# Last token block of a hybrid layer: mixer rows loaded early into a pool of their own, and the sums of its first weights made beside the early blocks

## The chip, the cores and the metric

The kernel runs on one core of a Trainium2 chip. The core has TensorE (PE, matrix multiply; PEld is its weight load), VectorE (DVE), ScalarE (ACT), GpSimd (POOL) and SyncE (SP), which here only issues DMAs. Each takes its instructions in order. Times are device microseconds of the whole kernel; lower is better.

## What is computed

One layer of a hybrid encoder on 17 tiles of up to 128 tokens (16 of the prompt, one of 64 sample tokens), model width 1024. Three mixers (Mamba-2, RWKV-7, HGRN2) scan the tokens in order; their joined output y goes through an output projection, then a SwiGLU feed-forward network (FFN):

```python
y = concatenate([y_ssd, y_rw, y_hg], axis=-1)
x = x + y @ w_out
h = rmsnorm(x, norm2_w)
x = x + (silu(h @ w_gate) * (h @ w_up)) @ w_down
out = rmsnorm(x, final_norm_w)
```

Every product is made of float32 values split into a high and a low part (hi, lo) of a reduced type, with three multiplies in place of one: hi·hi, lo·hi, hi·lo.

## The kernel before

**Blocks.** The projection and FFN run over blocks of tokens. Three early blocks of three tiles each (EARLY: 0-2, 3-5, 6-8; class Ffn) run out() (output projection, norm), ffn() (22 column groups f of gate, up and down) and rest() (the final norm of each tile). Beside them the mixers of later tiles are worked off as streams. The late block (LATE, eight tiles, halves h of four tiles j) comes after all mixers: it does its projections by one level of Strassen-Winograd, seven products (PRODS) of half-size sub-matrices in place of eight. Their right operands are quarters of the weights (b11 to b22) and sums of them (t1 to t4); their left ones are quarters of the rows (a11 to a22) and sums (s1 to s4).

**Order.** A scheduler in the build sets the order of instructions on each engine from the program and the dependencies of tiles. What can be placed early depends on the tiles' pools: a pool opened at the addresses of one that was closed waits for the last users of those addresses.

**Weights.** Weight units come through two small rings. "raw" has three tiles of 256 KB (128x512 float32), "w" five of 512 KB (hi and lo). The first early block splits the units and keeps them in DRAM; later blocks load them ready (w<-w, line 214). Sums of weights are made by t_sums (lines 1308 to 1327): four quarters are loaded into raw tiles on SP, summed, and the four results go to DRAM on POOL's queue. For the output projection ("wo", six groups) the program places them in the last early block (out_prep), for w_down ("wd", eleven) after each pair; both use POOL for the arithmetic. When needed, a sum is loaded again and split by parts().

**Late block, step by step.** After the last early block: the ya tiles (y of the three mixers, 24 loads, line 1427), the residual rows acc and the norm's row nw are loaded on SP. Op tiles (to_parts, lines 1405 and 1406: a copy on ACT and a subtraction on VectorE) feed the output projection, tokens_first("wo"). second_half works on the rows of the second half while the projection still runs, first_half(j) on those of the first: transposes (line 1464, d<-ident,w2k), sums and parts of them. Then come eleven pairs (gate and up columns): columns() yields after each of its seven products, x, y and z are PSUM banks, and c tiles hold copies and sums. Two pairs are stepped ahead by two products each. The results' seven combinations are stored (ms and ma, on POOL's queue). At the end m_group loads them into mraw for tokens_first("wd"), acc comes back from DRAM (xs), and final_norm writes the outputs.

final_norm (lines 1125 to 1136) squares a row on ACT into a w2k tile h, writes the normalised row over the same tile, and stores from there.

Of the kernel before, what the change touches and what calls it, by code (L numbers as in the profile page):

```python
# [19 lines left out]
P = 128  # L20
D = 1024
# [27 lines left out]
NH = 4  # L49
TAIL = 4  # L50
# [26 lines left out]
def body(tc, A, O, blocks=None, supers=None, dbg=None):  # L77
# [1047 lines left out]
    def final_norm(p, xt, t, n, fw, h):  # L1125

        s2 = mk(p, [P, 2], tag="s2", bufs=2)
        ss = mk(p, [P, 1], tag="ss", bufs=2)
        for hf in range(2):
            S.activation(h[hf][:n], xt[:, hf * 512:hf * 512 + 512], AF.Square, accum_out=s2[:n, hf:hf + 1])  # L1130
        V.tensor_tensor(ss[:n], s2[:n, 0:1], s2[:n, 1:2], ADD)
        rs = inv_rms(p, ss, n, 1, 1.0 / D, EPS)
        for hf in range(2):
            cs = slice(hf * 512, hf * 512 + 512)
            V.scalar_tensor_tensor(h[hf][:n], xt[:, cs], rs[:n], fw[:n, cs], MUL, MUL)
            G.dma_start(O["y_prompt"][(t - 1) * P:t * P, cs] if t else O["y_sample"][:, cs], h[hf][:n])

    class Ffn:
# [134 lines left out]
        def final(self, i, fw):  # L1273
            t, n = self.tiles[i], self.lens[i]
            final_norm(self.fp, self.acc[:n, i, :], t, n, fw, [self.w2k(), self.w2k()])

    if supers:
# [4 lines left out]
        def early():  # L1282
            drain(ALLY(EARLY[0]))
            fs[0].start()
            for i, f in enumerate(fs):
                drain(ALLY(EARLY[i]))
                yield from f.out()
                if i + 1 < len(fs):
# [3 lines left out]
                    yield from f.ffn(NFF - AHEAD, NFF)  # L1292
                else:
# [13 lines left out]
        def t_sums(key, q, p, tag, bufs, eng):  # L1307

            def ld(n):
                r = mk(p, [P, 512], tag=tag, bufs=bufs)  # L1310
# [8 lines left out]
            eng.tensor_tensor(a, a, b, SUB)  # L1319
            st("t3", a)  # L1320
            c_ = ld(0)
            eng.tensor_tensor(b, b, c_, SUB)
            st("t1", b)
            eng.tensor_tensor(c_, a, c_, ADD)
            st("t2", c_)
            d_ = ld(2)
            eng.tensor_tensor(d_, d_, c_, SUB)
            st("t4", d_)

        def quarters(key, kk):  # L1330
            if key == "wo":
# [9 lines left out]
        def parts(raw, eng):  # L1341
# [3 lines left out]
            eng.tensor_tensor(lo, raw, wt[:, 0], SUB)  # L1345
            return hi, lo

        def b_tm(key, kk, n):
# [5 lines left out]
            return parts(raw, V)  # L1354
# [5 lines left out]
        def tokens_first(key, order, per, group, acc, then, ahead, behind):  # L1360
# [3 lines left out]
            for a, b, x, fresh, (h, d) in PRODS:  # L1364
                if fresh:
                    banks[x] = [(xbank if x == 0 else ybank)() for _ in range(NH)]
                ps = banks[x]
                add = lambda j: V.tensor_tensor(acc[h][:, j, d * 512:d * 512 + 512], ps[j],
                                                acc[h][:, j, d * 512:d * 512 + 512], ADD)
# [12 lines left out]
                for g0 in range(0, len(order), per):  # L1382
                    kks = order[g0:g0 + per]
                    op = ops.get(g0) or group(a, kks)
                    for i, kk in enumerate(kks):
                        wu = b_tm(key, kk, b)
# [13 lines left out]
        def op_tile(tag="op"):  # L1400
            o = mk(lq, [P, 2, 4, 512], F32, tag=tag, bufs=4 if tag == "op" else 3)
# [5 lines left out]

        flow(early())
# [6 lines left out]
        lq = pool(st, "lq", side="right", reuse_waits="tile")  # L1415
        tile_of = lambda h, j: LATE[h][j]
        xs2 = [dram.tile([P, NH, D], F32, tag=f"xs{h}", name=f"xs{h}") for h in range(2)]

# [3 lines left out]
        ya = {}  # L1422
        for m in (2, 0, 1):
            ya[m] = mk(lq, [P, 2, 4, 512], F32, tag="ya", bufs=3)
            for h in range(2):
                for j in range(NH):
                    nc.sync.dma_start(ya[m][:, h, :, j * P:j * P + P], yscr[m][tile_of(h, j)])  # L1427
        acc = [mk(lo_, [P, NH, D], tag=f"acc{h}", bufs=1) for h in (1, 0)][::-1]
        for h in range(2):
# [26 lines left out]
        def scaled(h, j):  # L1456
            hs[h, j] = [mk(lo_, [P, 512], tag="w2k", bufs=4) for _ in range(2)]
            rms_scaled(lo_, acc[h][:, j, :], P, nw, hs[h, j])
            G.dma_start(xs2[h][:, j, :], acc[h][:, j, :])
# [55 lines left out]
        def columns(w, i):  # L1515

            raw = {}
            for n, f, k in (("22", 1, 1), ("12", 1, 0), ("11", 0, 0), ("21", 0, 1)):
                raw[n] = mk(lp, [P, 512], tag="lraw", bufs=16)
                nc.sync.dma_start(raw[n], w[2 * i + f][:, k * 512:k * 512 + 512])  # L1520
            V.tensor_tensor(raw["22"], raw["22"], raw["12"], SUB)
            V.tensor_tensor(raw["12"], raw["12"], raw["11"], SUB)
            V.tensor_tensor(raw["11"], raw["22"], raw["11"], ADD)
            V.tensor_tensor(raw["21"], raw["21"], raw["11"], SUB)
            raw = {"t3": raw["22"], "t1": raw["12"], "t2": raw["11"], "t4": raw["21"]}

            def prod(ps, a, b, first=True):
                if b in raw:
                    hi, lo = parts(raw[b], V)
                else:  # L1530
                    f, k = int(b[2]) - 1, int(b[1]) - 1
                    hi, lo = load_unit(w[2 * i + f][:, k * 512:k * 512 + 512])
# [7 lines left out]
            def copy(tag, ps):  # L1540
                r = mk(lp, [P, 512], tag=tag, bufs=4)
# [211 lines left out]
```

## Time and profile before

| | us |
|---|---|
| runs of the kernel, median of three | 3619.61 |
| lowest, highest | 3611.94, 3636.17 |
| profiled execution | 3608.43 |
| its span (mean clock 0.97) | 3606.7 |
| TensorE busy | 3373.3 |
| VectorE, ScalarE, GpSimd busy | 2199.1, 1238.1, 794.7 |

Times in a row of the profile are from the span's start. A row of the timeline has start, duration, engine, line, operation, output<-inputs, shapes, count, and in brackets the engine's idle time before it with what ended it. In rows of groups the part behind the bar is busy time and mean of one in ns. PEclk is the granted clock of TensorE as a share of full speed; DMA share is the load of the 16 DMA engines.

### The profile page before, as it was taken

What the parts mean: (1) busy time and instruction counts of PE and PEld (TensorE: products, weight loads), DVE (VectorE), ACT (ScalarE), POOL (GpSimd) and SP (SyncE); (2) the same over time, 40 slices, a digit from 0 to 9 for tenths busy, and PEclk for the clock granted to TensorE, in tenths of its full rate; (3) what the DMA queues carried; (4) which work ended last, traced back from release to release, by engine and by line L of the source; (5) the groups of instructions that cost most, each with busy time, mean ns of one, the idle gap of its engine ahead of it and who ended that gap; (6) DMA issues with size and microseconds to landing.
All of it is one profiled execution on the core that took longest, in us unless ns stands there. A gap on an engine that the chain in (4) does not pass through costs nothing.

```text
span 3606.7 us, 60714 instructions
## 1 busy us (share of the span) xinstructions
PE 3373.3 (94%) x22588; PEld 2951.2 (82%) x22588; DVE 2199.1 (61%) x4866; ACT 1238.1 (34%) x2618; POOL 794.7 (22%) x1048
## 2 busy tenths in 40 slices
PE   7999999999999998989888999999997969999798
PEld 7998689889799996778777889879996757888586
DVE  3358456558766677687776666766435775554353
ACT  4445333344433444434342222322102432333231
POOL 3325202102111123345444200111000343010001
PEclk9999999999999999899999999999999979999899
DMA  9776865555666668789888867777778678564756
GB/s 316 233 221 220 287 213 173 159 171 176 240 213 179 202 206 303 262 282 322 290 313 306 280 221 241 232 258 232 222 254 263 221 241 284 175 194 142 261 188 207
DMA packets 424256, 847.80 MB, mean 235 GB/s; under 512 B 111233, under 2 KB 211081, under 8 KB 419865
## 3 DMA queue, kind: packets, MB, share of 16 engines
q1 hardware_dynamic: 404024, 778.37, 65.8%
q0 software_dynamic: 19936, 65.55, 4.8%
q8 instruction: 178, 2.92, 0.3%
q14 instruction: 118, 0.96, 0.1%
HBM read 597.52 MB, written 246.25 MB: 234 GB/s over the span
## 4 chain that ended last, share of the span: by engine, by line
PE 43%; DMA 13%; issue 11%; DVE 8%; POOL 4%; SPq 2%; ACT 1%; POOLq 0%; DVEq 0%; ACTq 0%
PE g L109 32%; PE d L109 3%; PE c L109 3%; PE h L109 3%; DMA raw<-in_w_down 2%; DMA w<-w 2%; DMA raw<-in_w_gate 1%; POOL w L220 1%; DMA raw<-in_w_up 1%; DVE tp L638 1%; DVE Xp L639 1%; SPq L1427 1%; DMA raw<-in_w_out 1%; DMA b4k<-psc 1%; POOL ms L1599 1%
## 5 line engine op out<-in xcount | busy, mean ns | idle before, releaser
L109 PE MATMUL g<-hhi,w 128*128 128x384 f32 (+3 forms) x3312 | 833.6, 330 | 12.6 <-DMA w<-w 4.4
L109 PEld LDWEIGHTS g<-hhi,w 128*128 128x128 f32 (+1 forms) x3312 | 579.7, 188 | 28.5 <-DMA w<-w 4.1
L109 PE MATMUL g<-h2hi,w 128*128 128x384 f32 (+1 forms) x2112 | 544.0, 334 | 7.9 <-ACT w L218 3.3
L109 PE MATMUL g<-hlo,w 128*128 128x384 f32 (+3 forms) x1680 | 549.9, 328 | 0.0
L109 PEld LDWEIGHTS g<-h2hi,w 128*128 128x128 f32 x2112 | 374.6, 189 | 18.0 <-ACT w L218 4.8
L109 PE MATMUL g<-h2lo,w 128*128 128x384 f32 (+1 forms) x1056 | 349.1, 331 | 1.1 <-DVE h2lo L253 1.1
L220 POOL TENSOR_TENSOR w<-raw,w 128x512 fp32r<-128x512 f32 x180 | 247.9, 1380 | 343.4 <-ACT w L218 303.4
L109 PEld LDWEIGHTS g<-hlo,w 128*128 128x128 f32 (+1 forms) x1680 | 313.9, 187 | 6.0 <-issue 0.5
L109 PE MATMUL g<-w,mhi 128*128 128x512 f32 x792 | 262.6, 409 | 14.2 <-ACT w L218 7.0
L109 PE MATMUL g<-w,op 128*128 128x512 f32 x816 | 198.3, 403 | 45.9 <-ACT op L1405 42.2
L109 PEld LDWEIGHTS g<-w,op 128*128 128x128 f32 x816 | 156.1, 192 | 85.4 <-ACT op L1405 43.9
L218 ACT ACTIVATE w<-raw 128x512 fp32r<-128x512 f32 x240 | 149.7, 628 | 205.8 <-PE g L109 45.2
L109 PEld LDWEIGHTS g<-h2lo,w 128*128 128x128 f32 x1056 | 199.6, 189 | 5.2 <-DVE h2lo L253 1.8
L109 PEld LDWEIGHTS g<-w,mhi 128*128 128x128 f32 x792 | 149.4, 193 | 49.0 <-ACT w L218 8.4
L109 PE MATMUL g<-w,hhi 128*128 128x512 f32 (+1 forms) x544 | 179.6, 410 | 10.2 <-DMA w<-w 6.9
L109 PE MATMUL d<-op,w 128*128 128x512 f32 x792 | 185.5, 392 | 1.8 <-DMA w<-w 0.9
L109 PEld LDWEIGHTS d<-op,w 128*128 128x128 f32 x792 | 148.4, 188 | 35.5 <-issue 1.7
L638 DVE TENSOR_TENSOR tp<-Xp,b4k 128x60 f32<-128x60 f32 (+24 forms) x527 | 131.1, 249 | 74.2 <-DMA b4k<-psc 61.6
L1271 DVE TENSOR_TENSOR acc<-g,acc 128x512 f32<-128x512 f32 (+1 forms) x198 | 133.0, 684 | 43.3 <-PE g L109 42.8
L109 PE MATMUL g<-w,mlo 128*128 128x512 f32 x396 | 158.9, 402 | 0.0
L109 PE MATMUL d<-w,op 128*128 128x512 f32 x612 | 144.1, 395 | 0.0
L109 PEld LDWEIGHTS d<-w,op 128*128 128x128 f32 x612 | 115.1, 188 | 27.7
(425 smaller groups left out, 6232.7 us busy)
## 6 DMA issues: line engine op xcount, KB each, us to landing
w<-w SPq DMA_DIRECT2D x893, 512.0 KB, 4.3
raw<-in_w_down SPq DMA_DIRECT2D x88, 256.0 KB, 4.2
hin<-hg SPq DMA_DIRECT2D x16, 1280.0 KB, 6.2
rin<-rw SPq DMA_DIRECT2D x16, 896.0 KB, 5.8
hg<-stage SPq DMA_DIRECT2D x64, 192.0 KB, 2.9
raw<-in_w_out SPq DMA_DIRECT2D x48, 256.0 KB, 4.1
sin<-ss SPq DMA_DIRECT2D x16, 768.0 KB, 5.2
raw<-in_w_gate SPq DMA_DIRECT2D x44, 256.0 KB, 4.7
```

The costliest lines, as they stand in the source:

```text
L109: return T.matmul(out, lhsT, rhs, start=start, stop=stop, skip_group_check=more)
L218: S.activation(hi, raw, AF.Copy)
L220: (G if units[0] % 4 < GLO else V).tensor_tensor(lo, raw, wt[:, 0], SUB)
L638: V.tensor_tensor(tv, _bc(Xp[:, 0:m, q], 2, w), _bc(Up[:, q, q + 1:32], 1, m), MUL)
L639: V.tensor_tensor(Xp[:, 0:m, q + 1:32], Xp[:, 0:m, q + 1:32], tv, ADD)
L1271: V.tensor_tensor(self.acc[:n, i, cs], ps[:n], self.acc[:n, i, cs], ADD)
L1427: nc.sync.dma_start(ya[m][:, h, :, j * P:j * P + P], yscr[m][tile_of(h, j)])
L1599: G.dma_start(msc[n, g][:, k, :], r)
```

## The change

- **ya early.** The last early block's ffn is cut at column group 14 (SWITCH). There the mixers are drained and their pools closed; a pool of its own (lqa) opens in their place, and the 24 ya loads are issued, after them columns 14 to 21 and rest(). The op tiles stay in a pool (lq) that opens behind the block.
- **Rows on another queue.** acc and nw of the late block, and acc and fw at the end, come row tile by row tile on POOL's queue.
- **Sums of the first weights.** prep_sums runs as a stream after the second block's out(). It makes the sums of wo and also those of w_gate and w_up for pairs 0 to 2 (PRE). All sums, those of wd too, are made by VectorE. Pairs 0 to 2 load their sums from DRAM (b_part).
- **Products ahead.** Pairs 0 to 2 (six matrices) are stepped ahead by two products. Their x and y banks both come from xbank (four g banks); in these pairs x is a new bank in the product s4.
- **Final norm in place.** The normalised rows are written over acc and stored from it; the squares go to a tile of their own.
- **End.** The first group of mraw is asked for ahead of acc and fw.

```diff
-    def final_norm(p, xt, t, n, fw, h):
+    def final_norm(p, xt, t, n, fw):
...
-            S.activation(h[hf][:n], xt[:, hf * 512:hf * 512 + 512], AF.Square, accum_out=s2[:n, hf:hf + 1])
+            dump = mk(p, [P, 512], tag="w2k", bufs=4)
+            S.activation(dump[:n], xt[:, hf * 512:hf * 512 + 512], AF.Square, accum_out=s2[:n, hf:hf + 1])
...
-            V.scalar_tensor_tensor(h[hf][:n], xt[:, cs], rs[:n], fw[:n, cs], MUL, MUL)
-            G.dma_start(O["y_prompt"][(t - 1) * P:t * P, cs] if t else O["y_sample"][:, cs], h[hf][:n])
+            V.scalar_tensor_tensor(xt[:, cs], xt[:, cs], rs[:n], fw[:n, cs], MUL, MUL)
+            G.dma_start(O["y_prompt"][(t - 1) * P:t * P, cs] if t else O["y_sample"][:, cs], xt[:, cs])
...
                 yield from f.out()
+                if i == 1:
+                    streams.append(Stream(prep_sums(), 1.0))
                 if i + 1 < len(fs):
...
-                    streams.append(Stream(out_prep(), 1.0))
-                    yield from f.ffn(0, NFF)
-                yield from f.rest()
+                    yield from f.ffn(0, SWITCH)
...
-            eng.tensor_tensor(a, a, b, SUB)
+            V.tensor_tensor(a, a, b, SUB)
...
-        def out_prep():
-            for kk in (4, 5, 0, 1, 2, 3):
-                t_sums(f"wo{kk}", quarters("wo", kk), ring, "raw", RB, G)
-                yield 40.0
+        def prep_sums():
+            for key, kks in (("wo", (4, 5, 0, 1, 2, 3)), ("w_gate", range(PRE)), ("w_up", range(PRE))):
+                for kk in kks:
+                    t_sums(f"{key}{kk}", quarters(key, kk))
+                    yield 35.0
...
         flow(early())
         drain(ALLY(range(NT)))
         stA.close()
-        stE.close()
...
+        lqa = pool(st, "lqa", side="right", reuse_waits="tile")
         ya = {}
         for m in (2, 0, 1):
-            ya[m] = mk(lq, [P, 2, 4, 512], F32, tag="ya", bufs=3)
+            ya[m] = mk(lqa, [P, 2, 4, 512], F32, tag="ya", bufs=3)
             for h in range(2):
                 for j in range(NH):
                     nc.sync.dma_start(ya[m][:, h, :, j * P:j * P + P], yscr[m][tile_of(h, j)])
...
+        flow(fs[-1].ffn(SWITCH, NFF))
+        flow(fs[-1].rest())
+        stE.close()
+        lq = pool(st, "lq", side="right", reuse_waits="tile")
...
-                nc.sync.dma_start(acc[h][:, j, :], x_rows(tile_of(h, j))[0][0])
-        nw = norm_rows(lo_, "norm2")
+                G.dma_start(acc[h][j], x_rows(tile_of(h, j))[0][0])
+        nw = mk(lo_, [P, D], tag="nw", bufs=1)
+        G.dma_start(nw, A["norm2"].partition_broadcast(P))
...
             x = xbank()
             prod(x, "s1", "t1")
-            c22 = copy("c22", x)
+            c22 = copy("c22", x, 6)
             yield
-            y = ybank()
+            y = xbank() if pre else ybank()
             prod(y, "a22", "t4")
...
-            prod(x, "s4", "b22", False)
+            if pre:
+                add(c12, c22)
+                x = xbank()
+            prod(x, "s4", "b22", pre)
...
-        pairs = [Pair(0), Pair(1)]
-        for _ in range(2):
-            for p_ in pairs:
-                p_.step()
+        pairs = [Pair(i) for i in range(PRE)]
+        for p_ in pairs:
+            p_.step()
+            p_.step()
...
-            t_sums(f"wd{i}", quarters("wd", i), ring, "raw", RB, G)
+            t_sums(f"wd{i}", quarters("wd", i))
...
-        for h in (1, 0):
-            nc.sync.dma_start(acc[h], xs2[h])
-        fw = norm_rows(l2, "fw")
...
+        ahead_ = m_group("a11", range(4))
+        for h in range(2):
+            for j in range(NH):
+                G.dma_start(acc[h][j], xs2[h][j])
+        G.dma_start(fw, A["fw"].partition_broadcast(P))
```

How the order of instructions moves, at three places. On SP's queue before, at the start of the late block, the first of 24 ya loads (y is the mixers' output in DRAM), behind the first weight units of the output projection (w<-w):

```order
L214 DMA w_29148<-w_15673 128x1024
L214 DMA w_29165<-w_15737 128x1024
L214 DMA w_29179<-w_15759 128x1024
L214 DMA w_29196<-w_15841 128x1024
L1427 DMA ya_29086<-y_9_199 128x4x128
L1427 DMA ya_29086<-y_10_200 128x4x128
L1427 DMA ya_29086<-y_11_201 128x4x128
```

and behind the last of them the residual rows, the norm's row and the next weight:

```order
L1427 DMA ya_29104<-y_15_188 128x4x128
L1427 DMA ya_29104<-y_16_189 128x4x128
L1431 DMA acc_4188_29114<-in_x_prompt 128x1024 x4
L1431 DMA acc_4187_29113<-in_x_prompt 128x1024 x4
L148 DMA nw_29123<-in_norm 128x1024
L214 DMA w_29210<-w_15857 128x1024
```

On SP's queue after, the same loads stand between weights of the last early block's FFN:

```order
L216 DMA w_28063<-w_18486 128x1024
L216 DMA w_28078<-w_18519 128x1024
L1430 DMA ya_28364<-y_9_199 128x4x128
L216 DMA w_28092<-w_18567 128x1024
L1430 DMA ya_28364<-y_10_200 128x4x128
L1430 DMA ya_28364<-y_11_201 128x4x128
L1430 DMA ya_28364<-y_12_202 128x4x128
L216 DMA w_28112<-w_18600 128x1024
L1430 DMA ya_28364<-y_13_203 128x4x128
L1430 DMA ya_28364<-y_14_204 128x4x128
L1430 DMA ya_28364<-y_15_205 128x4x128
L216 DMA w_28114<-w_18607 128x1024
```

They moved ahead of the FFN's last third, some three between two weights; acc and nw are on POOL's queue now.

On TensorE before, behind the output projection of the late block, the last transposes of first_half (d<-ident,w2k) and then pair 0's first products (g<-ya,w: ya_29841 is a tile of parts, w a weight's part):

```order
L1464 MATMUL d_30080<-ident,w2k_29989 128x128 x4
L1464 MATMUL d_30093<-ident,w2k_29990 128x128 x4
L1464 MATMUL d_30116<-ident,w2k_30015 128x128 x4
L1464 MATMUL d_30129<-ident,w2k_30016 128x128 x4
L1464 MATMUL d_30152<-ident,w2k_30098 128x128 x4
L1464 MATMUL d_30165<-ident,w2k_30099 128x128 x4
L1464 MATMUL d_30175<-ident,w2k_30134 128x128 x4
L1464 MATMUL d_30188<-ident,w2k_30135 128x128 x4
L109 MATMUL g_30214<-ya_29841,w_30215 128x512 x12
L109 MATMUL g_30244<-ya_29841,w_30245 128x512 x12
```

On TensorE after, at the same place:

```order
L1476 MATMUL d_30215<-ident,w2k_30124 128x128 x4
L1476 MATMUL d_30228<-ident,w2k_30125 128x128 x4
L111 MATMUL g_30337<-ya_29976,w_30340 128x512
L111 MATMUL g_30357<-ya_29976,w_30360 128x512
L111 MATMUL g_30377<-op_29975,w_30380 128x512 x12
L111 MATMUL g_30397<-op_29975,w_30400 128x512 x10
L1476 MATMUL d_30251<-ident,w2k_30150 128x128 x4
L1476 MATMUL d_30264<-ident,w2k_30151 128x128 x4
L111 MATMUL g_30337<-ya_29976,w_30340 128x512 x9
L1476 MATMUL d_30287<-ident,w2k_30233 128x128 x4
L111 MATMUL g_30337<-ya_29976,w_30340 128x512 x2
L111 MATMUL g_30357<-ya_29976,w_30360 128x512 x10
```

The four first products of pair 0 (g_30337, g_30357, g_30377, g_30397) now stand among the transposes; the products of the next pair follow behind the last transpose.

On SP at the end of the pairs before (xs are the residual rows kept in DRAM, nw the final norm's row):

```order
L214 DMA w_33571<-w_18592 128x1024
L1620 DMA acc_4821_33496<-xs_29082 128x4096
L1620 DMA acc_4820_33495<-xs_29081 128x4096
L148 DMA nw_33499<-in_fw 128x1024
L1626 DMA mraw_33505<-ma_30059 128x2048
L1626 DMA mraw_33566<-ma_30060 128x2048
```

and after:

```order
L216 DMA w_33687<-w_18198 128x1024
L216 DMA w_33706<-w_18600 128x1024
L1638 DMA mraw_33627<-ma_30194 128x2048
L1638 DMA mraw_33701<-ma_30195 128x2048
L1638 DMA mraw_33762<-ma_30196 128x1536
```

The rows and the norm's row are gone from SP, and mraw follows the weights directly.

More of the change, by code (lines that the diff above doesn't have):

```diff
@@ L1274, in final @@
             t, n = self.tiles[i], self.lens[i]
-            final_norm(self.fp, self.acc[:n, i, :], t, n, fw, [self.w2k(), self.w2k()])
+            final_norm(self.fp, self.acc[:n, i, :], t, n, fw)
     if supers:
@@ L1292, in early, with t_sums @@
                     yield from f.ffn(NFF - AHEAD, NFF)
+                    yield from f.rest()
                 else:
-                    streams.append(Stream(out_prep(), 1.0))
-                    yield from f.ffn(0, NFF)
-                yield from f.rest()
+                    yield from f.ffn(0, SWITCH)
         tdram = {}
-        def t_sums(key, q, p, tag, bufs, eng):
+        def t_sums(key, q):
             def ld(n):
-                r = mk(p, [P, 512], tag=tag, bufs=bufs)
+                r = mk(ring, [P, 512], tag="raw", bufs=RB)
                 nc.sync.dma_start(r, q[n])
@@ L1353, in b_tm @@
             nc.sync.dma_start(raw, tdram[f"{key}{kk}", n])
-            return parts(raw, V)
+            return parts(raw)
         PRODS = [("a11", "b11", 0, True, (0, 0)), ("s3", "t3", 1, True, (1, 1)), ("s2", "t2", 0, False, (1, 0)),
@@ L1406, in to_parts @@
             V.tensor_tensor(lo, src, hi.bitcast(F32), SUB)
+        tile_of = lambda h, j: LATE[h][j]
+        xs2 = [[dram.tile([P, D], F32, tag=f"xs{h}{j}", name=f"xs{h}{j}") for j in range(NH)] for h in range(2)]
         flow(early())
@@ L1513, in body, with columns @@
         stF = ExitStack()
-        def columns(w, i):
+        def columns(key, i):
+            q = dict(zip(("b11", "b12", "b21", "b22"), quarters(key, i)))
             raw = {}
[L1518 to L1525, printed above, removed]
-            def prod(ps, a, b, first=True):
[L1528 to L1532, printed above, removed]
+            if i >= PRE:
+                for n in ("b22", "b12", "b11", "b21"):
+                    raw[n] = mk(lp, [P, 512], tag="lraw", bufs=8)
+                    nc.sync.dma_start(raw[n], q[n])
+                b11, b12, b21, b22 = (raw[n] for n in q)
+                V.tensor_tensor(b22, b22, b12, SUB)
+                V.tensor_tensor(b12, b12, b11, SUB)
+                V.tensor_tensor(b11, b22, b11, ADD)
+                V.tensor_tensor(b21, b21, b11, SUB)
+                raw = {"t3": b22, "t1": b12, "t2": b11, "t4": b21}
+            def prod(ps, a, b, first=True):
+                hi, lo = parts(raw[b]) if b in raw else b_part(key, i, b)
                 ah, al = hop[a]
@@ L1555, in columns @@
             prod(z, "a11", "b11")
-            c11 = copy("c11", z)
+            c11 = copy("c11", z, 4)
             yield
@@ L1604, in body @@
         lp = pool(stF, "lp", reuse_waits="tile")
-        pairs = [Pair(0), Pair(1)]
-        for _ in range(2):
-            for p_ in pairs:
-                p_.step()
+        pairs = [Pair(i) for i in range(PRE)]
+        for p_ in pairs:
+            p_.step()
+            p_.step()
         for i in range(NFF // 2):
-            if i > 1:
+            if i >= PRE:
                 pairs.append(Pair(i))
             pairs[i].finish()
-            t_sums(f"wd{i}", quarters("wd", i), ring, "raw", RB, G)
+            t_sums(f"wd{i}", quarters("wd", i))
         stF.close()
         l2 = pool(st, "l2", reuse_waits="tile")
-        acc = [mk(l2, [P, NH, D], tag=f"acc{h}", bufs=1) for h in range(2)]
-        for h in (1, 0):
-            nc.sync.dma_start(acc[h], xs2[h])
-        fw = norm_rows(l2, "fw")
+        mraw = lambda: mk(l2, [P, 4, 512], tag="mraw", bufs=2)
         def m_group(name, kks):
             n = len(kks)
-            raw = mk(l2, [P, 4, 512], tag="mraw", bufs=2)
+            raw = mraw()
             nc.sync.dma_start(raw[:, :n], msc[name, kks[0] // 4][:, :n])
@@ L1631, in finish @@
         def finish(h, j):
-            final_norm(l2, acc[h][:, j, :], tile_of(h, j), P, fw, [mk(l2, [P, 512], tag="w2k", bufs=4) for _ in range(2)])
+            final_norm(l2, acc[h][j], tile_of(h, j), P, fw)
         def rows_done(a):
@@ L1637, in rows_done @@
                     finish(1, j)
-        tokens_first("wd", list(range(NFF // 2)), 4, m_group, acc, rows_done, lambda prepare: None, lambda j: finish(0, j))
+        acc = [[mk(l2, [P, D], tag=f"acc{h}{j}", bufs=1) for j in range(NH)] for h in range(2)]
+        fw = mk(l2, [P, D], tag="nw", bufs=1)
+        ahead_ = m_group("a11", range(4))
[3 more added lines that the diff above has]
+        G.dma_start(fw, A["fw"].partition_broadcast(P))
+        tokens_first("wd", list(range(NFF // 2)), 4, lambda n, kks: ahead_ if (n, kks[0]) == ("a11", 0) else m_group(n, kks), acc, rows_done, lambda prepare: None, lambda j: finish(0, j))
         st.close()
```

50 lines of the change are left out of this document (26 added, 24 removed).

## The prediction

> **What bounds the kernel now.** I read the page's totals first, then what TensorE waited for late in the span.
>
> ```profile
> span 3606.7 us, 60714 instructions
> PE 3373.3 (94%) x22588; PEld 2951.2 (82%) x22588; DVE 2199.1 (61%) x4866; ACT 1238.1 (34%) x2618; POOL 794.7 (22%) x1048
> ...
> engine line waited for: us in total, times, longest us
> PE g L109 <- ACT op L1405: 42.2, 4, 25.2
> PE d L1464 <- DVE w2k L244: 19.1, 4, 7.1
> PE g L109 <- ACT w L1344: 13.7, 1, 13.7
> PE g L109 <- DMA w<-w: 10.6, 3, 5.3
> ```
>
> TensorE (PE) is busy for 3373 of 3607 us, so time can only come out of its idle stretches. The waits are those from 2350 us to the end. Only the first three rows (75 us) are touched by the change, and the timeline of PE shows three places:
>
> ```profile
> start us, us, engine line op out<-in xcount [idle before <-releaser]
> 2731.19 0.39 PE L109 MATMUL g<-w,mlo 128*128 128x512 f32 x1
> 2747.02 8.07 PE L109 MATMUL g<-w,op 128*128 128x512 f32 x24 [15.44 <-ACT op L1405]
> 2755.28 5.86 PE L109 MATMUL g<-w,op 128*128 128x512 f32 x24 [0.19 <-ACT op L1405]
> ...
> 2777.65 3.07 PE L109 MATMUL g<-w,op 128*128 128x512 f32 x12 [3.68 <-DMA w<-w]
> ...
> 2873.57 3.05 PE L109 MATMUL g<-w,op 128*128 128x512 f32 x12
> 2880.74 3.27 PE L1464 MATMUL d<-ident,w2k 128*128 128x128 f32 x16 [4.12 <-DVE w2k L244]
> ...
> 2916.74 11.67 PE L109 MATMUL g<-ya,w 128*128 128x512 f32 x38 [13.66 <-ACT w L1344]
> ...
> 3344.06 5.66 PE L109 MATMUL d<-ya,w 128*128 128x512 f32 x24
> 3374.91 10.25 PE L109 MATMUL g<-w,op 128*128 128x512 f32 x33 [25.19 <-ACT op L1405]
> ```
>
> Gap 1 (2731.6 to 2777.7) is the start of the late block, gap 2 (2876.6 to 2916.7) lies between its out-projection and its first gate/up pair, gap 3 (3349.7 to 3374.9) between the last pair and the down projection.
>
> **Gap 1, the loads of ya.** In 46.1 us PE did 96 of these multiplies (24+24+8+8+4+28 in the timeline), 5.86 us for 24, so 23 us of work: 23 us are lost. The cause is in the loads' rows and in ACT's timeline:
>
> ```profile
> L1427 SPq DMA_DIRECT2D ya<-y x24: 594/832/2834, 2732.7 to 2759.2; - x24
> L1405 ACT ACTIVATE op<-ya x11: 1042/1045/1062, 2745.9 to 2795.3; 128x1024 fp32r<-128x1024 f32 x11
> ...
> 2739.72 0.63 ACT L1130 ACTIVATE w2k<-acc 128x512 f32<-128x512 f32 x1 [8.80 <-DMA out_y_prompt<-w2k]
> ```
>
> The 24 loads start only after the FFN's last multiply, and the last squares of the final norm wait on ACT for a store of the tile they overwrite. Afterwards ya lies in SBUF long before; the first op tile still takes the place of the FFN's m tiles, so it waits for the last down multiply. Left on the path are that add (0.7), two squares that no longer wait for a store (0.63 each, with a short read behind each, 1.6 in all), one op copy (1.05) and semaphores: 4.3 us, and the first 24 multiplies again cold (8.07 against 5.86: 2.2). Loss 6.5 in place of 23: **gain 17** (13 to 20; the acc rows now come on POOL's queue behind the last stores and are needed only with the first products' sums, about 20 us later).
>
> **What these 24 loads cost inside the FFN.** The order shows them three to one among eight weight loads, on the SP queue. The stretch they move into:
>
> ```profile
> core 0: us, PE busy (x) PEld busy (x) DVE busy (x) ACT busy (x) POOL busy (x), PEclk, DMA share, GB/s
> 1960.00:2040.00 80.00, 75.75 (x503) 68.87 (x501) 54.32 (x111) 20.66 (x43) 33.14 (x33) 0.96 0.87 288
> ...
> 2600.00:2650.00 50.00, 50.00 (x267) 47.04 (x266) 14.80 (x24) 4.07 (x8) 0.00 (x0) 1.00 0.80 256
> ...
> 2731.00:2747.00 16.00, 0.58 (x3) 0.15 (x1) 5.13 (x12) 2.50 (x5) 4.49 (x8) 0.62 1.01 307
> 2747.00:2778.00 31.00, 25.75 (x98) 19.75 (x99) 20.69 (x19) 7.71 (x9) 0.00 (x0) 0.92 1.12 350
> ...
> L214 SPq DMA_DIRECT2D w<-w x24: 319/319/320, 2600.9 to 2648.7; - x24
> ```
>
> PE is full there and takes a 512 KB weight unit every 2.1 us (24 in 50 us). 24 loads of 256 KB and 8 units are 10.5 MB: 34 us at the 307 GB/s of the first window in which ya came, 30 at the 350 of the second. PE uses 8 units in 17 us, and the ring of five covers some four more, 8 us. So it stalls 5 to 9 us, and the first ya load can hold the weights behind it on SP while it waits for the last mixer's store. **Cost 8** (0 to 18). By the Trainium skill ("DMA: Bandwidth & Descriptors", Where 436 GB/s comes from) HBM gives a core about 358 GB/s; an estimate from that figure is 29 us of loading and a cost of 4. The 350 of the second window agrees, the 307 of the first, where ya came alone at full share, does not, and I keep the rows.
>
> **Gap 2, first_half and the first products.** In 40.1 us PE had only transposes. VectorE sets the pace, and not at its own speed:
>
> ```profile
> 2876.00:2917.00 41.00, 8.25 (x36) 5.95 (x35) 39.36 (x56) 15.79 (x31) 21.52 (x25) 0.57 0.62 213
> ...
> L1406 DVE TENSOR_TENSOR op<-hraw,op 128x512 fp32r<-128x512 f32 x9 | 10.7, 1192 | 0.0
> L244 DVE SCALAR_TENSOR_TENSOR w2k<-acc,rs,nw 128x512 f32<-128x512 f32 x8 | 8.1, 1055 | 0.5 <-POOL rs L228 0.5
> ...
> L1406 DVE TENSOR_TENSOR ya<-hraw,ya 128x512 fp32r<-128x512 f32 x4 | 2.7, 680 | 0.0
> ...
> L1327 POOL TENSOR_TENSOR raw<-raw,raw 128x512 f32<-128x512 f32 x3 | 3.9, 1303 | 2.7 <-DMA raw<-in_w_down 2.7
> ```
>
> The same subtraction takes 680 ns in one group and 1192 in another, while POOL makes the sums of w_down beside it. Against 680 the two slow groups lose 9×0.51 + 8×0.37 = 7.6 us. The change takes these sums off POOL and out of this place, and pair 0's own sums (four at 0.69, 2.8 us) too, but adds the low parts of the early products. The order now has 47 large VectorE instructions from the end of the out-projection to the end of first_half: 47×0.68 = 32 us, of which about one runs before. So PE has its steady work 31 us after the out-projection instead of 40.1: 9 us. Second, it fills part of the 31: pair 0's four products (48 multiplies, 5.66 us for 24, so 11.2) stand among the transposes. Pairs 1 and 2 do not get in: all six matrices now take both banks from the four g banks, and ACT's copies that free them stand behind first_half's. **Gain 20** (9 if nothing gets in, 37 if all 144 multiplies do; nearest to the four products that need no bank back).
>
> The Trainium skill ("SBUF — State Buffer", Two separate sides) says that a VectorE instruction with two SBUF inputs and a GpSimd one that reads SBUF exclude each other for a whole instruction. The trace agrees in direction; by that rule each of the nine POOL sums here (three in the row, two in each of the three groups beside it) could hold VectorE for its 1.3 us, 12 us instead of 7.6, and the gain would be 24.
>
> **Gap 3, the last pair to the down projection.** The chain that ended last reads there:
>
> ```profile
> 3354.48 13.10 DMA ms<-c
> ...
> 3367.84 5.09 DMA mraw<-ma
> ...
> 3372.95 1.92 ACT op L1405
> ...
> ms<-c POOLq DMA_DIRECT2D x44, 256.0 KB, 6.1
> ```
>
> The last store took 13.1 us beside 4 MB of acc rows that SP had just issued; the median of such a store is 6.1. Now these rows go on POOL's queue, behind the stores. mraw lies where the last pair's c tiles were, so it still waits for that store, on SP with only down weights queued behind it: 3354.5 + 6.1 + 5.1 + 1.9 and half a microsecond of issue is 3368.1, and I leave 1 for acc rows beside mraw. **Gain 6** (0 to 9).
>
> **Block 1, the sums made early.** Six sums (w_out) were already made there on POOL; now twelve are, on VectorE: 48 instructions of 0.69, 33 us between about 1880 and 2150, where VectorE is busy for 54.3 of 80 us in the window above, against 24 POOL sums that no longer slow it. Six new ones bring 24 loads and 24 stores, 12.6 MB in about 120 us. What PE and POOL lost to the first six:
>
> ```profile
> PE g L109 <- DMA w<-w: 0.6, 3, 0.2
> ...
> POOL raw L1327 <- DMA raw<-in_w_out: 19.4, 5, 6.6
> POOL raw L1319 <- DMA raw<-in_w_out: 15.5, 4, 6.7
> POOL raw L1322 <- DMA raw<-in_w_out: 13.5, 5, 5.4
> ```
>
> PE lost 0.6 us to weights from 1960 to 2040 with DMA share 0.87, so the loads are nearly hidden. But the sums' wait for their loads, 48.4 us on POOL where little was queued behind, now stands in VectorE's queue: behind it stand the mixers' steps and the FFN's m tiles, for which PE waits in turn. When I put the sums' places in the new order beside the times that their neighbours and the loads have in the trace of before, the first three sums find their loads landed, and the next three would wait 2 to 6 us an instruction; PE has banks in reserve: **cost 4** (0 to 15 inside the forecast). Normalising in place of the final norm takes ACT's wait for stores away and gives the next block's acc loads one; I put it at 0 (-3 to 3).
>
> **The pairs.** The sums of w_down, 44 instructions of 0.69 (30 us), now stand in VectorE's queue among the pairs:
>
> ```profile
> 3050.00:3300.00 250.00, 250.00 (x1094) 205.13 (x1093) 128.74 (x201) 77.16 (x130) 25.84 (x48) 1.00 0.56 183
> ```
>
> VectorE is half idle there and PE never waits, so PE's steady work covers them; without that cover they cost their 30 us and their loads' waits. **Cost 1** (0 to 10).
>
> **Sum.** 17 + 20 + 6 - 8 - 4 - 1 = 30 less. The profiled execution took 3608.4 us, 11 less than the median of the runs (3619.6, from 3611.9 to 3636.2), so 3578 by it and **3589** as a median.
>
> **Rivals.** *VectorE waits for the sums' loads* (slower): at the rate of POOL's 48.4 for six sums, twelve hold VectorE 97 us. It makes the change a loss once PE loses 34 of it (the 43 of gain less the 9 of other costs); if three quarters reach PE (73), the time is 3619.6 - 43 + 9 + 73 = 3659. For it: in-order queues, raw ring of three, each sum needing three loads. Against: VectorE idles a third of that stretch, and the order puts a sum 20 us after the last. *The FFN pays for ya*: the loads move the stall, cost 20 instead of 8: 3601. *The filling doesn't happen*: products of pair 0 stand late for their sums from DRAM, gap 2 gains 9: 3600. *All of it is hidden*: gap 2 fills wholly (37) and the FFN pays nothing: 3619.6 - 60 + 5 = 3565.
>
> **How the numbers follow.** One per cent is 36 us, about what a measurement of this kernel can tell from no change. Forecast 0.50 (its own bounds put somewhat under half of it beyond 36 less), FFN pays 0.12, no filling 0.12, all hidden 0.14, VectorE waits 0.12. Faster by over 1%: 0.22 + 0.14 and 0.04 of the others, 0.40; slower by over 1%, the greater part of the last case, 0.09; within 1%: 0.51. The range reaches 13 us beyond the hidden case and 10 above no change, and leaves out most of the slow case: 3552 to 3630.
>
> **What would show it.** Gap 1 of some 5 us before the first g<-w,op; ya loads inside the FFN with PE waiting for w<-w there; VectorE's op<-hraw back at 680 ns; 48 g<-ya or g<-op multiplies among the L1464 transposes; ms<-c near 6 us at the end. I am wrong if PE waits for VectorE between 1900 and 2200, or if gap 2 keeps over 30 us idle.

## The result, and the profile after

The changed kernel takes 3584.57 us (median of four runs, 3574.35 to 3585.44), the kernel before, in four runs, 3616.72: a ratio of 0.9892 with a 95% interval from 0.9856 to 0.9927. The prediction said 3589; the time lies in its range, on the edge between "faster by over 1%" and "within 1%". The profiled execution of the changed kernel has a span of 3582.0 us, 24.7 less than before. All stage lengths below are from these two executions.

The page's totals and TensorE's waits late in the span, after:

```profile
span 3582.0 us, 60919 instructions
PE 3376.5 (94%) x22588; PEld 2950.8 (82%) x22588; DVE 2200.1 (61%) x4940; ACT 1237.6 (35%) x2618; POOL 727.5 (20%) x1022
...
engine line waited for: us in total, times, longest us
PE g L111 <- ACT op L1412: 22.1, 2, 19.0
PE d L111 <- DMA w<-w: 11.5, 6, 3.5
PE g L111 <- DMA w<-w: 10.9, 7, 2.6
PE g L111 <- ACT c L1553: 10.0, 1, 10.0
PE g L111 <- ACT ya L1412: 3.0, 1, 3.0
```

The waits for op tiles fell from 42.2 to 22.1 us, those of transposes for w2k (19.1) are nearly gone, and waits for weights rose from 13.5 to 22.4. The new row is ten microseconds for a c copy on ACT. Where they stand, from TensorE's timeline:

```profile
start us, us, engine line op out<-in xcount [idle before <-releaser]
2590.87 0.73 PE L111 MATMUL g<-w,mhi 128*128 128x512 f32 x2 [1.56 <-DMA w<-w]
2595.82 0.70 PE L111 MATMUL g<-w,mhi 128*128 128x512 f32 x2 [2.62 <-DMA w<-w]
...
2743.73 18.52 PE L111 MATMUL g<-w,op 128*128 128x512 f32 x72 [3.10 <-ACT op L1412]
...
2870.45 1.22 PE L111 MATMUL g<-ya,w 128*128 128x512 f32 x2 [3.04 <-ACT ya L1412]
2871.47 7.62 PE L111 MATMUL g<-op,w 128*128 128x512 f32 x22
...
2899.00 8.06 PE L111 MATMUL g<-ya,w 128*128 128x512 f32 x24 [10.04 <-ACT c L1553]
...
3114.47 10.09 PE L111 MATMUL d<-op,w 128*128 128x512 f32 x36 [3.52 <-DMA w<-w]
...
3348.89 28.01 PE L111 MATMUL g<-w,op 128*128 128x512 f32 x108 [19.00 <-ACT op L1412]
```

Gap 1 is 3.1 us. In gap 2 pair 0's products run from 2870 on, then TensorE waits for a bank. Gap 3 is 19.0 us. The marks in the table are starts of the FFN's residual adds on VectorE (198 of them in three early blocks; the 1st, 132nd, 151st and 195th) and starts and ends of groups in TensorE's timeline. The FFN's last multiply ends 3.4 us after the 195th add in both.

| stage, us | before | after | change | forecast |
|---|---|---|---|---|
| to the first add (nothing changed acts here) | 1527.1 | 1529.8 | +2.7 | 0 |
| to block 1's last add (132nd) | 811.8 | 809.8 | -2.0 | +4 |
| to block 2's 19th add (151st) | 226.8 | 221.9 | -4.9 | 0 |
| to its 63rd add (195th), three before its last: ya in the FFN | 162.5 | 175.7 | +13.2 | +8 |
| last FFN multiply to end of output projection | 145.0 | 125.9 | -19.1 | -17 |
| from there to the last pair's last multiply | 473.1 | 463.3 | -9.8 | -20 + 1 |
| gap 3 | 25.2 | 19.0 | -6.2 | -6 |
| down projection and the rest | 231.8 | 233.1 | +1.3 | 0 |

The first row differs though the code there is the same: over all kernels run here it lies between 1519.9 and 1533.4, and the second between 806.9 and 816.6 for kernels with the same instructions in it. Single runs of whole kernels therefore tell little below ten microseconds. The later stages repeat better: in experiments 1 and 10, whose instructions stand in the changed kernel's order up to the end of the pairs, the FFN's stage takes 176.2 and 175.9 us and the output projection's 127.1 and 125.8, but the stage to the last pair takes 461.2 and 459.5 where the changed kernel has 463.3. A difference of four microseconds in that stage is not told from chance.

### The profile page after: what moved, and what is told of

Its sections match the earlier page's. It is cut to its first block, busy times and chain, and to the rows that moved or that the text cites. A ratio compares the mean times of both kernels' runs of the same rounds, so it can differ in the third digit from the quotient of the medians.

```text
span 3582.0 us, 60919 instructions
## 1 busy us (share of the span) xinstructions
PE 3376.5 (94%) x22588; PEld 2950.8 (82%) x22588; DVE 2200.1 (61%) x4940; ACT 1237.6 (35%) x2618; POOL 727.5 (20%) x1022
## 4 chain that ended last, share of the span: by engine, by line
PE 29%; issue 13%; DMA 6%; DVE 5%; POOL 3%; ACT 1%; SPq 1%; POOLq 0%; DVEq 0%; ACTq 0%
PE g L111 21%; PE d L111 4%; DMA w<-w 2%; PE h L111 2%; PE c L111 1%; DMA raw<-in_w_down 1%; DMA raw<-in_w_gate 1%; POOL w L222 1%; DMA raw<-in_w_up 1%; POOL ms L1614 1%; POOL ma L1614 0%; DMA raw<-in_w_out 0%; DVE acc L1274 0%; DVE tp L640 0%; DVE Xp L641 0%
## 5 line engine op out<-in xcount | busy, mean ns | idle before, releaser
L111 PE MATMUL g<-w,op 128*128 128x512 f32 x816 | 197.0, 401 | 22.1 <-ACT op L1412 22.1
L111 PEld LDWEIGHTS g<-w,op 128*128 128x128 f32 x816 | 155.5, 191 | 61.1 <-ACT op L1412 23.0
L111 PE MATMUL d<-op,w 128*128 128x512 f32 x720 | 170.4, 395 | 8.2 <-DMA w<-w 8.2
L111 PEld LDWEIGHTS d<-op,w 128*128 128x128 f32 x720 | 136.0, 189 | 39.7 <-issue 9.8
```

The source lines that it names most:

```text
L111: return T.matmul(out, lhsT, rhs, start=start, stop=stop, skip_group_check=more)
```

## The experiments

All are edits of the changed kernel. Each was profiled; all but two were run once, and the two with several timed runs are marked.

**1. The point at which the FFN is cut.**

```diff
-SWITCH = 14
+SWITCH = 22
```

> The changed kernel with SWITCH = 22: the whole FFN of the last early block runs ahead of the ya loads, everything else of the change stays. Theory A (the 24 loads, wherever they stand, are the cost): TensorE's waits for weights in the FFN's last third (8.6 us in the changed kernel) are gone, and the late block starts with 12 us or more of waiting and about 20 us lost in all, as before; the kernel is some 8 to 12 us slower than the changed one. Rival B (gap 1 was closed by the final norm in place, which took ACT's wait for a store away): the first wait stays at 3 to 5 us, and the kernel is some 9 us faster than the changed one.

Neither theory was tested: the order did not move on any engine, so this run repeats the changed kernel. The ya loads still stood between the weights of the FFN's last third (six waits from 1.13 to 2.53 us there, 3.10 in gap 1), in 3580.9 us. By the next experiment, what lets the scheduler place them early is the pool of their own at the mixers' addresses, not the place of the statement.

**2. ya in one pool with op again.**

```diff
-        lqa = pool(st, "lqa", side="right", reuse_waits="tile")
+        flow(fs[-1].ffn(SWITCH, NFF))
+        flow(fs[-1].rest())
+        stE.close()
+        lq = pool(st, "lq", side="right", reuse_waits="tile")
+        lqa = lq
         ya = {}
...
-        flow(fs[-1].ffn(SWITCH, NFF))
-        flow(fs[-1].rest())
-        stE.close()
-        lq = pool(st, "lq", side="right", reuse_waits="tile")
```

> The changed kernel with ya and op tiles in one pool that opens behind the last early block, as before (the column group at which the FFN is cut had moved nothing: the pool's place does); the final norm in place, the rows on POOL's queue, the sums and the early products stay. Theory A (the place of the 24 loads is gap 1): TensorE's waits for weights in the FFN's last third (8.6 us) are gone; from the FFN's last multiply to the end of the output projection it takes 138 to 145 us as before (145.0), against 125.9 in the changed kernel; the kernel is 4 to 12 us slower than the changed one. Rival B (the final norm in place and the rows on the other queue closed gap 1): this stage takes under 131 us.

The FFN's stage is back at 162.5 us without a wait for weights, and the output projection's takes 155.5, 29.6 more than in the changed kernel: theory A, and more than it asked for. In this kernel's TensorE timeline and SP's loads:

```profile
2759.89 7.91 PE L111 MATMUL g<-w,op 128*128 128x512 f32 x24 [28.26 <-ACT op L1412]
...
2732.96 38.79 SPq L1434 DMA_DIRECT2D ya<-y  x24
...
2733.00:2760.00 27.00, 0.11 (x1) 0.11 (x1) 3.12 (x8) 1.78 (x3) 8.58 (x16) 0.51 1.05 360
```

ACT's last square starts at 2733.0 in it, since no store is waited for, and yet TensorE waits till 2759.9: SP issues the 24 loads over 38.8 us instead of some 27 (2732.7 to 2759.2 before), while POOL's queue issues the acc rows from 2737.6 to 2744.6 (the last number of the window: 360 GB/s). So the final norm in place closed nothing here by itself; that the rows on the other queue make ya later still fits these times, and was not tried alone. The early ya is worth 29.6 - 13.2 = 16 us in this kernel; against the kernel before, whose rows came after ya, 19.1 - 13.2 = 6.

**3. ya in four groups over the rest of the FFN, on POOL's queue.**

```diff
-            for h in range(2):
-                for j in range(NH):
-                    nc.sync.dma_start(ya[m][:, h, :, j * P:j * P + P], yscr[m][tile_of(h, j)])
-        flow(fs[-1].ffn(SWITCH, NFF))
+        todo = [(m, h, j) for m in (2, 0, 1) for h in range(2) for j in range(NH)]
+        for f in range(SWITCH, NFF, CF):
+            for m, h, j in todo[:6]:
+                if f > SWITCH:
+                    S.activation(ya[m][:, h, 0, j * P:j * P + 1], fs[-1].due[2][:, 0, 0:1].bitcast(F32), AF.Copy)
+                G.dma_start(ya[m][:, h, :, j * P:j * P + P], yscr[m][tile_of(h, j)])
+            todo = todo[6:]
+            flow(fs[-1].ffn(f, f + CF))
```

> The changed kernel with the 24 ya loads on POOL's queue, six ahead of each of the FFN's last four steps of two columns: a one-element copy from the step before into each load's place holds the last 18 back (six one-element copies on ACT per step are added; the loads overwrite the element). Theory A (24 loads in 28 us beside the weights are more than the DMA engines and the ring of five units carry; bandwidth): TensorE's waits for weights in the FFN's last third fall from 8.6 us to 3 or less. Rival B (any of these loads holds weights up, however spread): the waits stay at 6 us or more, over a longer stretch. The output projection's stage stays at 125 to 128 us in both.

The loads stand from 2577 to 2694, in four bursts of six, each issued in 4.4 us, and the stage takes 176.2 us, as with the one burst (175.7). The waits for weights are 7.6 us, in six places, each some 7 to 15 us behind the start of a burst. By these numbers it is rival B.

```profile
L1433 POOL DMA_DIRECT2D ya<-y x24: 747/747/763, 2576.8 to 2694.4; - x24
...
2577.00:2613.00 36.00, 35.04 (x188) 32.63 (x187) 9.71 (x16) 3.20 (x7) 4.23 (x6) 1.00 0.85 287
2613.00:2705.00 92.00, 85.31 (x420) 77.25 (x419) 25.10 (x41) 8.53 (x31) 13.31 (x18) 0.94 0.81 271
...
2644.60 1.22 PE L111 MATMUL g<-w,mhi 128*128 128x512 f32 x2 [2.66 <-DMA w<-w]
...
2703.64 0.74 PE L111 MATMUL g<-w,mhi 128*128 128x512 f32 x2 [2.03 <-DMA w<-w]
```

These loads are not in SP's queue, so the cost does not need weights that stand behind them in that queue. But within a burst they come faster than in the changed kernel (six in 4.4 us, there 24 in some 28), so whether loads that are spread evenly would be cheaper was not tried, and theory A is not refuted: the run shows that four bursts cost as much as one.

**4. The sums of w_down back on POOL, in the same places.**

```diff
-        def t_sums(key, q):
+        def t_sums(key, q, V=V):
...
-            t_sums(f"wd{i}", quarters("wd", i))
+            t_sums(f"wd{i}", quarters("wd", i), G)
```

> The changed kernel with the eleven sums of w_down back on POOL, at the same places in the queues; everything else stays. In the changed kernel TensorE waits 10.1 us for weights between 3050 and 3340, which it did not before. Theory A (SP stands at the lraw loads, since lraw has 8 tiles in place of 16, and weights queue behind): the waits stay at 8 to 12 us. Rival B (VectorE waits in its queue for the sums' loads, 53 us in the trace, and so releases raw and lraw tiles late): the waits fall to 3 us or less. In either case VectorE's sums beside POOL's get slower than 690 ns.

The waits for weights stay (12.3 us from 2900 to 3330): VectorE's queue is not their cause. The stage takes 470.5 us, 7.1 more than in the changed kernel; about half of that comes from a slower pace of multiplies late in this run (last section), and the rest is no more than the stage's spread.

**5. Twelve lraw tiles in place of eight.**

```diff
-                    raw[n] = mk(lp, [P, 512], tag="lraw", bufs=8)
+                    raw[n] = mk(lp, [P, 512], tag="lraw", bufs=12)
```

> The changed kernel with 12 lraw tiles in place of 8 (16 as before do not fit). Theory A (SP stands at the lraw loads): TensorE's waits for weights between 3050 and 3340 fall from 10.1 us to 4 or less, and SP's wait at these loads for VectorE falls from 112 us. Rival B (VectorE's order with the sums): they stay at 8 to 12 us.

(lraw tiles hold the quarters of gate and up weights that the pairs' sums are made of.) The waits from 2900 to 3330 fall only from 11.5 to 8.6 us, and the stage takes 461.3, as in experiment 1. Theory A explains little of it: SP's wait at these loads fell from 112.2 to 97.2 us, and in the kernel before, where weights were on time, it had been 165.5.

**6. No early sums of gate and up, nothing ahead.**

```diff
-PRE = 3
+PRE = 0
```

> The changed kernel with PRE = 0: no sums of w_gate and w_up in the second early block, no products stepped ahead of the first pair; ya early, sums on VectorE and the rest stay. Theory A (the early products are worth the multiplies they put among the transposes): between output projection and steady pairs TensorE idles for some 30 us, 11 to 16 us more than in the changed kernel, and nothing is gained in the second early block (within 3 us); the kernel is 11 to 18 us slower than the changed one. Rival B (most of gap 2's gain is POOL's sums being gone, and the early sums cost in the second block what they give): within 4 us of the changed kernel.

Both readings hold in part. Gap 2 is 39.0 us without a product in it (40.1 before): its whole gain goes with the early sums and products. But the stage to the last pair takes 466.8, only 3.5 more than in the changed kernel (7.3 more than the shortest of the same order), since the pairs run almost without waits for weights (1.7 us). Of the 44 loads for its sums of w_down this kernel issues half before the end of gap 2 (13 before it, 9 in it) and the last at 3005, and pair 0's own sums stand in the gap too, on VectorE; the changed one, whose three raw tiles serve the early products there, issues all 44 among the pairs, from 2928 to 3140:

```profile
L1315 SPq DMA_DIRECT2D raw<-in_w_down x44: 327/328/695, 2928.2 to 3139.6; - x44
...
core 0: us, PE busy (x) PEld busy (x) DVE busy (x) ACT busy (x) POOL busy (x), PEclk, DMA share, GB/s
2850.00:2900.00 50.00, 35.61 (x168) 28.69 (x167) 43.83 (x81) 33.38 (x73) 7.37 (x10) 0.83 0.29 101
2950.00:3150.00 200.00, 190.27 (x813) 154.28 (x812) 123.96 (x198) 54.61 (x96) 43.91 (x81) 0.98 0.83 284
```

That gave a new theory, C: the DMA engines are at a share of 0.29 while TensorE waits and of 0.83 in the pairs, and the sums' transfers there make the weights late. A high share alone does not: this kernel, with the rest of its sums among the pairs, has a share of 0.85 from 2950 to 3000 and TensorE busy for 49.40 of the 50 us.

```profile
2950.00:3000.00 50.00, 49.40 (x216) 40.23 (x215) 34.64 (x56) 14.35 (x25) 11.00 (x21) 1.00 0.85 299
```

**7. The sums of w_down made early too.**

```diff
-            for key, kks in (("wo", (4, 5, 0, 1, 2, 3)), ("w_gate", range(PRE)), ("w_up", range(PRE))):
+            for key, kks in (("wo", (4, 5, 0, 1, 2, 3)), ("w_gate", range(PRE)), ("w_up", range(PRE)), ("wd", range(NFF // 2))):
...
-                    yield 35.0
+                    yield 35.0 if key != "wd" else 15.0
...
-            t_sums(f"wd{i}", quarters("wd", i))
```

The rest of the edit runs the stream to its end before the late block.

> The changed kernel with the eleven sums of w_down made by the same stream as the first weights' sums, behind those, beside the early blocks, and no longer among the pairs. Theory C (the sums' 88 transfers of 256 KB slid out of the idle stretch ahead of the pairs into the first half of the pairs, DMA share 0.82 to 0.86, and there make the weights late): TensorE's waits for weights from 2900 to 3330 fall from 11.5 us to 3 or less, and the stage from the end of the output projection to the last pair takes 450 to 455 us in place of 463.3; the early blocks lose 0 to 6 us. Rival D (SP held at the lraw loads alone): the waits stay over 8 us.

No wait for weights is left among the pairs, and the stage takes 445.4 us, 14 to 18 less than in the three kernels of the same order there.

```profile
2950.00:3150.00 200.00, 200.00 (x876) 164.09 (x875) 106.64 (x166) 59.75 (x101) 22.15 (x41) 1.00 0.59 195
```

The early blocks pay as much or more, where 0 to 6 were expected: from block 1's last add to block 2's 63rd 406.8 us against 397.6, and the part before 824.6 against 809.8 (806.9 to 816.6 in kernels with the same instructions). So the sums cost 14 to 18 us beside the pairs and 17 to 27 beside the early blocks.

**8. Only one of the eleven sums.**

```diff
-            nc.sync.dma_start(raw, tdram[f"{key}{kk}", n])
+            nc.sync.dma_start(raw, tdram["wd0" if key == "wd" else f"{key}{kk}", n])
...
-            t_sums(f"wd{i}", quarters("wd", i))
+            if i == 0:
+                t_sums("wd0", quarters("wd", 0))
```

> The changed kernel with only the first of the eleven sums of w_down made; the down projection loads this one wherever it needs a sum, so ten sums' 80 transfers and their arithmetic are left out and the output is not the layer's. It prices the sums themselves. Theory C (their transfers make the pairs' weights late, wherever they stand they cost about that): the stage from the end of the output projection to the last pair takes 443 to 448 us in place of 463.3, as when the sums were moved ahead, and the FFN of the last early block keeps its 175.7 us, where the moved sums made the early blocks longer; the kernel is 15 to 20 us faster than the changed one. Rival D (SP held at the lraw loads for VectorE): waits for weights from 2900 to 3330 stay over 6 us, and the stage stays over 455 us.

No wait for weights in the pairs, and the FFN's stage is unchanged (176.6). The stage takes 453.5 us, 9.9 less, and the kernel 3571.85, some 12 less: both short of what theory C asked for. In this run all multiplies of the pairs stood 1.9% farther apart (109 in 25 us against 111), an estimated 8 us over the stage, without which it would be near the 445 of the run before. The share of the DMA engines in the same window of this kernel:

```profile
2950.00:3150.00 200.00, 200.00 (x859) 161.98 (x858) 105.79 (x165) 59.11 (x100) 22.13 (x41) 1.00 0.59 199
```

From 0.83 to 0.59, and TensorE busy throughout. That the sums make the weights late is shown: without them no wait is left, here and in the run before, though SP waits longer for lraw tiles here (161.8 us) than in the changed kernel (112.2). How they do it is not. Besides the share of the DMA engines, these runs take away the sums' turns in SP's queue, where a load of a quarter waits for one of three raw tiles, and weights stand behind it. In the changed kernel five of the six late weights were issued right behind such a load, and the sixth behind the load of a finished sum, which had waited for the last sum's store; ahead of the longest wait (3.52 us, to 3114.47) two such loads hold SP for 3.30 us, where a free one takes 0.33:

```profile
3104.10 3.30 SPq L1315 DMA_DIRECT2D raw<-in_w_down  x2
3107.50 0.40 SPq L216 DMA_DIRECT2D w<-w  x1
```

The transfers are slower too: from 2950 to 3150 a weight lands 6.5 us after its issue in the changed kernel, 4.2 in experiment 7 and 4.3 here (medians). Which of the two counts for more was not separated.

**9. The second products' banks.**

```diff
-            y = xbank() if pre else ybank()
+            y = ybank()
```

> The changed kernel with the second product's bank of pairs 0 to 2 taken from the d banks, as before, so that four g banks hold the first products of two pairs and d banks, free behind the last transpose, take the second ones. Theory A (products of the next pairs wait for banks, which ACT's copies behind first_half's copies free): the single wait for ACT's copy (10.0 us in the changed kernel) falls to 4 us or less, and 4 to 8 us are gained up to the last pair. Rival B (the pairs' parts and weights set the pace, not the banks): the wait only changes its name, and under 2 us are gained.

The wait of 10.0 us is gone; what is left there is 1.8 and 0.6 for VectorE's hraw (sums of the transposed rows):

```profile
2895.70 3.00 PE L111 MATMUL d<-op,w 128*128 128x512 f32 x12 [0.60 <-DVE hraw L1507]
2900.51 7.34 PE L111 MATMUL d<-op,w 128*128 128x512 f32 x24 [1.81 <-DVE hraw L1515]
```

The stage takes 452.8, 7 to 10 less than in the kernels of the same order. Theory A, with somewhat more than it promised.

**10. The final rows behind mraw.**

```diff
-                G.dma_start(acc[h][j], xs2[h][j])
-        G.dma_start(fw, A["fw"].partition_broadcast(P))
+                nc.sync.dma_start(acc[h][j], xs2[h][j])
+        nc.sync.dma_start(fw, A["fw"].partition_broadcast(P))
```

> The changed kernel with the final stage's acc rows and norm row on SP again, behind the first mraw load. In the changed kernel this mraw load takes 9.6 us beside the rows on POOL's queue; before, alone, 5.1. Theory A (the rows beside it slow it): the load takes 5 to 6.5 us and TensorE's wait ahead of the down projection falls from 19.0 to 15 or 16 us. Rival B (the load is slow for another reason, its reads or its place in the queue): the wait stays at 18 to 20 us, or the second group, now behind 4 MB of rows, takes the gain away again.

The chain that ended last in the changed kernel, ahead of the down projection:

```profile
3334.04 3.17 DMA ms<-c
...
3337.34 9.56 DMA mraw<-ma
...
3346.93 1.92 ACT op L1412
```

The wait falls from 19.0 to 14.77 us, and the down projection gives 0.9 of it back (219.3 against 218.4). Theory A.

**11. Nine and ten together (five runs).** 

> The changed kernel with two of the edits already run together: the second products' banks from the d banks, and the final rows on SP behind the first mraw load. Theory (the two act in different stages and add): 10.5 us less from the end of the output projection to the last pair and 3.3 less from there to the end, so 3567 to 3574 against the changed kernel's 3584.6, with a ratio to the kernel before of 0.985 to 0.989. Rival (what the pairs gain is given back by the weights, which are already late there): under 7 us gained.

3571.78 us, median of five runs (3556.83 to 3576.53), 0.9854 of the kernel before with an interval from 0.9831 to 0.9877: the fastest version here. The stages add: 450.8, 14.8 and 219.2. The interval overlaps the changed kernel's; that it is faster, by some 12 to 16 us, rests on these stages.

**12. And the sums early (four runs).** 

> The kernel of banks and rows with the sums of w_down made early as well. Theory C (the sums' transfers among the pairs are what makes their weights late): the stage up to the last pair gets 14 to 18 us shorter again, the early blocks pay 6 to 12 for the same transfers, and the kernel takes 3558 to 3570. Rival (with the pairs started earlier the early blocks' loss weighs more): no faster than the kernel of banks and rows.

3575.98 us (3573.21 to 3577.36), 0.9878 (0.9862 to 0.9895). The stage to the last pair takes 434.9, 15.8 less than with nine and ten alone, and it is given back ahead: 406.5 against 396.9 from block 1's last add to block 2's 63rd, 6.7 before that and 2.3 in the output projection, 18.6 in all where 6 to 12 were expected. The rival.

## Why the prediction was right, point by point

**Gap 1** was forecast at 17 and gave 19.1. The first wait is 3.1 us where I had 4.3. ACT's wait for the store, which I named beside the loads, is no cause by itself: experiment 2 takes it away and the gap stays as long as the loads.

**ya in the FFN** was put at 8 and is 13.2. The waits are 8.6 us (8.0 for weights, 0.6 for a w2k tile), within the 5 to 9 forecast; most of the rest goes with the clock, which I had left out of this term. The window of these waits, changed kernel:

```profile
2577.00:2613.00 36.00, 27.36 (x122) 22.63 (x121) 7.48 (x12) 2.04 (x4) 0.00 (x0) 0.91 1.06 319
```

The granted clock is 0.91 in it and 1.00 from 2613 to 2705; 0.09 of 36 us is an estimated 3.2. The Trainium skill ("TensorE: Matmul & The Clock Gate", What's actually happening) puts the drop at an idle window of some 3.4 us; here no single wait is longer than 2.6, and the clock fell all the same.

**Gap 2** was right in both halves by size. From the end of the output projection to steady work it is 32.5 us, 7.7 shorter (9 forecast), and the 48 multiplies stand in it as the order said, 11.0 us at 0.229 each: 21.5 lost in place of 40.1, a gain of 18.7 against the 20 of the sum. VectorE is back at its pace:

```profile
L1413 DVE TENSOR_TENSOR op<-hraw,op 128x512 fp32r<-128x512 f32 x9 | 6.2, 684 | 0.1
```

684 ns where it was 1192 (the other slow group, w2k, came back to 748, not to the 680 of the working). The banks were the limit to the filling, as assumed, and experiment 9 shows their price. That VectorE's pace gave the first half is not shown. In experiment 6 the same subtraction takes 678 ns in the gap, and the gap stays at 39.0: two sums of w_down and pair 0's own sums stand in it, and it ends with 17.0 us of waiting for a weight that ACT copies. What shortens it is that these sums leave; which of them counts was not separated.

**The pairs** are the term that failed: cost 1 (0 to 10), measured 9 (18.7 us lost beside the 1848 multiplies and the gap, against 9.8 before; 5 to 9 with experiments 1 and 10, which have the same order). I asked who makes the sums and found VectorE half idle. The question was when their transfers run: with the raw tiles busy for the early products they left the idle gap for the first half of the pairs (experiments 6 to 8).

**Block 1** was to cost 4. The extra sums cost nothing that can be told from the spread; 4.9 us were gained at the change to block 2. There the kernel before waits 5.28 us for one weight, and the changed one twice, 0.88 and 2.02. The final norm in place does not do this by itself: experiment 6 has it too, waits 4.92 us for one weight there and takes 231.4 us in that stage, 9.5 more than the changed kernel. The cause stays open. The slower rival, VectorE waiting for the sums' loads, did not come: no row of waits for VectorE in those blocks exceeds 2.3 us.

**Gap 3** gave 6.2 of the 6, by errors that cancel: the store took 3.2 us instead of the 6.1 assumed, and mraw 9.6 beside the rows instead of 6.1.

The rows sum to -25 by the profiles, and the medians to -32: the executions ahead of the change differ by several microseconds from run to run, so the sum of 30 lies between two measurements of the same thing. That it came so close is in part luck: the FFN and the pairs took 13 us more than their terms, and the two stages of block 1 and the change to block 2 gave 11 more than theirs (+4 forecast, -6.9 measured), 6 of them in a stage that differs by 10 from run to run and 5 without a known cause.

## What to carry to other kernels

A transfer that is moved away from a stall is paid for where it lands: beside stages at a DMA share of 0.8, 6 MB cost 13 us whether in one burst or in four, and the sums of w_down with their 23 MB 14 to 18 beside the pairs and 17 to 27 beside the early blocks. Ask of every moved step which transfers slide along because it holds their buffers, what stands behind it in the same queue, and look for the stretch in which the DMA engines idle too. When a stall is filled with other work, the next limit is what that work needs to be released, here a PSUM bank whose copy stood behind the stall's own instructions.

## What the runs showed of the hardware beyond this

In three of the fourteen kernels profiled (4, 8 and 9) the pairs' multiplies stood 0.233 us apart in place of 0.229 (430 or 431 in place of 439 from 3200 to 3300), at a granted clock of 1.00, in two of them only from about 3150 on, while the down projection kept its 216 in 50 us (compared in these three and the changed kernel). No cause was found; it is worth up to 8 us of a stage, so stages are compared only after counting multiplies per window. In experiment 9 it hides an estimated 3 us more of gain.
